# One layer with a linear recurrence on one core: keys loaded once, and the output of a pair of chunks given to the scheduler before the front of the next

## The chip, the cores and the metric

The kernel runs on one core of a Trainium2 chip. The core has a matrix engine (TensorE, in the profile PE, with its weight loads as PEld), a vector engine (VectorE, DVE), an engine for activations and copies (ScalarE, ACT), a general engine (GpSimd, POOL) and an engine that here only issues DMA transfers (SyncE, SP). Each engine works through its own queue in order; engines wait for each other through semaphores. Data lie in device memory (DRAM), in the on-chip SBUF of 128 partitions, and in PSUM, where TensorE writes its products, in banks of 512 float32 values a partition.

The metric is the device time of one execution in microseconds (us): less is better. Before the change the median of three runs is 2554.62 us, from 2553.71 to 2556.13.

## The reference

One layer of a streaming encoder for 2048 tokens of width 1024, all in float32: token mixing, cross-attention into 256 memory tokens, and a feed-forward part, each between norms. Token mixing has one input projection, whose columns go to two groups of heads: a sliding-window attention and a gated linear recurrence. The change is in the recurrence, four heads of 128 by 128 state, in chunks of 64 tokens:

```python
    f = lbf + (1.0 - lbf) * jax.nn.sigmoid(f_logit.astype(f32))
    kf = 1.0 - f
    logf = jnp.log(f)
    b = jnp.cumsum(lc, axis=3)                       # within a chunk
    A = jnp.einsum('bhnqd,bhnkd->bhnqk', qc * jnp.exp(b - b_mid), kc * jnp.exp(b_mid - b))
    A = jnp.where(causal, A, 0.0)
    o_intra = jnp.einsum('bhnqk,bhnkv->bhnqv', A, vc)
    kv = jnp.einsum('bhnkd,bhnkv->bhndv', kc * jnp.exp(b_last - b), vc)
    # S_t = decay * S_{t-1} + kv, one chunk after the other
    o_inter = jnp.einsum('bhnqd,bhndv->bhnqv', qc * jnp.exp(b), S_prev)
    o = rms_norm(o_intra + o_inter, onorm_g) * jax.nn.silu(g)
```

Then follow the output projection, the cross-attention and the feed-forward part, which fill the time from about 790 us on.

## The kernel before

**Stages.** The input projection writes its result to DRAM (`z_d`), in two halves of 1024 tokens. The recurrence reads it back in pairs of chunks, 128 tokens at a time, 16 pairs in all. Pairs 0 to 7 run in a first pass beside the window attention (`swa`) and the input projection of the second half (`in_proj`, loop over `next(swa)`, `next(hgrn)`, `next(cols)`). Pairs 8 to 15 run in a second pass: the first step near the end of the attention, the others beside `fold_cross`, which multiplies the cross-attention's weights with each other and with the memory tokens; each step of the recurrence is followed by two steps of the fold. The results of both groups of heads go to `y_d`, which the output projection reads later, block after block of 256 tokens.

**One pair** goes through four functions.

- `hgrn_front` loads the keys twice (`k1` and `kk`, both 128x512), the queries (`qq`) and the values (`v`). GpSimd makes a scaled copy of the second chunk's queries (L890). TensorE multiplies keys with queries, eight matmuls into two banks (L897); VectorE and ScalarE take them out under the causal mask into `at` (L898, L899). GpSimd scales the queries for the state (`q6`, L902; the profile calls it q) and, in place, half of the second copy of the keys (`kk`, L905). TensorE transposes `kk` (L908) and `v` (L913) into a bank each, and ScalarE copies them to `kt` and `vt` (L910, L915).
- `hgrn_state` multiplies `kt` with `vt` (L924), GpSimd decays the old state into a new tile (L925), VectorE adds (L926). It returns the state from before.
- `hgrn_out` loads the gate (`sg`), adds `at` times values and queries times the earlier state in one bank (L936, L937), ScalarE sums the squares (L941), GpSimd makes the norm's factor of them (L943, L945: a power), and VectorE multiplies it on (L946), which frees the bank.
- `hgrn_last` transposes the normed output (L954), VectorE applies gain and gate (L955), and SP stores it.

`hgrn` is the loop over them. A step of it gives, in this order: the state of the last pair, the front of the next pair, the last part of the pair before the last, and the output of the last pair.

**Buffers.** `k1`, `kk`, `v` and `kt` have one buffer each, `qq`, `q6`, `at`, `vt` and the state `W` two. In the first pass all banks of the recurrence are the two of kind "h"; in the second, the kinds "g" and "t" with two each: state, first half of the attention products, key transposes and last part take "g", the second half, the value transposes and the output take "t". The fold uses "s" and "h".

**What sets the order.** The program is given to a scheduler, which follows a time line of its own and hands each engine its instructions in the order in which it expects them to be ready; of several that are ready it takes the one given first. So the order in the program is a priority, and a load is issued as soon as its buffer is free. On the chip each queue then runs strictly in that order. All loads and stores here go through `load` and `store`, on SP's queue (L75, L78).

Of the kernel before, what the change touches and what calls it, by code (L numbers as in the profile page):

```python
# [15 lines left out]
ALU = mybir.AluOpType  # L16
AX = mybir.AxisListType

P = 128
# [14 lines left out]
C_KA, C_VA, C_QH, C_FH, C_IH, C_GH = 512, 640, 768, 1280, 1792, 2304  # L34
# [14 lines left out]
class Layer:  # L49
# [144 lines left out]
    def mix(self):  # L194
        tc, I = self.tc, self.I
        kw = dict(reuse_waits="tile")
        with contextlib.ExitStack() as left:
# [18 lines left out]
            with tc.tile_pool(name="sw", bufs=1, side="right", **kw) as self.sw:  # L216
                self.zero_tiles()
                swa = self.swa(range(NT), lambda n: "st" if n < NPB else "sth")
                hgrn = self.hgrn(range(NPB), "h")
                cols = self.in_proj(1, u)  # L220
                next(cols)
                for _ in range(NPB + 1):
                    next(swa)
                    next(hgrn)
                    next(cols)
                for _ in hgrn:
                    pass
                self.out_sums, side = self.sums("out_s", self.w_out, 4, lambda: self.io_tile("u"), lambda: self.io_tile("x"))
                side = side()
                next(side)  # L230
                pairs = self.hgrn(range(NPB, NT), "gt")
                for i, _ in enumerate(swa, NPB + 2):
                    next(cols)
                    if i == NT + 1 - 0:
                        next(pairs)
                    for _ in range(4):
                        next(side, None)
# [168 lines left out]
    def zero_tiles(self):  # L406
# [19 lines left out]
        self.vst_prev = None  # L426
        self.W = ph.tile([P, 4, P], F32, tag="W", name="W0", bufs=2)
        nc.gpsimd.memset(self.W, 0.0)

# [437 lines left out]
    def hgrn_front(self, n, kinds):  # L867
        nc, ph = self.nc, self.hg
        t0 = n * P
        z = self.z_d  # L870
        kinds = itertools.cycle(kinds)

        def get(t, c):
            self.load(t, z[c:c + 512, t0:t0 + P].rearrange("(h p) t -> p h t", p=P))
            return t

        def new(tag, bufs=1, w=P):
            return ph.tile([P, 4, w], F32, tag=tag, name=f"{tag}{n}", bufs=bufs)

        def c8(ap):  # L880
            return ap.rearrange("p h (c t) -> p (h c) t", t=64)

        k1 = get(new("k1"), C_FH)
        qq = new("qq", 2, 192)
        q1 = get(qq[:, :, 0:P], C_QH)
        kk = get(new("kk"), C_FH)
        v = get(new("v"), C_IH)
        g1 = self.G1[:, n, :].unsqueeze(2).broadcast_to([P, 4, 64])

        nc.gpsimd.tensor_tensor(qq[:, :, P:192], qq[:, :, 64:P], g1, ALU.mult)  # L890

        at = self.atz[n % 2]
        for i in range(2):
            ps = self.bank(next(kinds))[:, 0:384].rearrange("p (h t) -> p h t", h=2)
            hs = slice(2 * i, 2 * i + 2)
            for r in range(2):
                nc.tensor.matmul(ps[:, r, :], k1[:, 2 * i + r, :], qq[:, 2 * i + r, :], start=True, stop=True)  # L897
            nc.vector.copy_predicated(at[:, hs, :], self.cmask.unsqueeze(1).broadcast_to([P, 2, P]), ps[:, :, 0:P])  # L898
            nc.scalar.activation(at[0:64, hs, 64:P], ps[0:64, :, P:192], AF.Copy)  # L899

        q6 = new("q6", 2)
        nc.gpsimd.tensor_tensor(q6.rearrange("p h (c t) -> p h c t", t=64), q1.rearrange("p h (c t) -> p h c t", t=64),  # L902
                                self.G[:, n, :, :].unsqueeze(3).broadcast_to([P, 4, 2, 64]), ALU.mult)

        nc.gpsimd.tensor_tensor(kk[:, :, 0:64], kk[:, :, 0:64], g1, ALU.mult)  # L905
        ps = self.bank(next(kinds))
        for h in range(4):
            nc.tensor.transpose(ps[:, h * P:(h + 1) * P], kk[:, h, :], self.ident)  # L908
        kt = new("kt")
        nc.scalar.activation(kt, ps.rearrange("p (h t) -> p h t", h=4), AF.Copy)  # L910
        ps = self.bank(next(kinds))
        for h in range(4):
            nc.tensor.transpose(ps[:, h * P:(h + 1) * P], v[:, h, :], self.ident)  # L913
        vt = new("vt", 2)
        nc.scalar.activation(vt, ps.rearrange("p (h t) -> p h t", h=4), AF.Copy)  # L915
        return q6, at, kt, vt

    def hgrn_state(self, n, kinds, kt, vt):
        nc, ph = self.nc, self.hg
        prev = self.W  # L920
        W = self.W = ph.tile([P, 4, P], F32, tag="W", name=f"W{n}", bufs=2)
        ps = self.bank(kinds[0])
        for h in range(4):
            nc.tensor.matmul(ps[:, h * P:(h + 1) * P], kt[:, h, :], vt[:, h, :], start=True, stop=True)  # L924
        nc.gpsimd.tensor_tensor(W, prev, self.G[:, n, :, 1].unsqueeze(2).broadcast_to([P, 4, P]), ALU.mult)  # L925
        nc.vector.tensor_tensor(W, ps.rearrange("p (h t) -> p h t", h=4), W, ALU.add)  # L926
        return prev

    def hgrn_out(self, n, kinds, q6, at, vt, W):
        nc, ph = self.nc, self.hg  # L930
# [28 lines left out]
    def hgrn(self, pairs, kinds):  # L959

        f, o = {}, {}
        for n in itertools.chain(pairs, (None, None)):
            if f:
                m, (q6, at, kt, vt) = f.popitem()
                W = self.hgrn_state(m, kinds, kt, vt)
            else:
                m = None
            if n is not None:
                f[n] = self.hgrn_front(n, kinds)
            if o:  # L970
                l, v = o.popitem()
                self.hgrn_last(l, kinds, *v)
            if m is not None:
                o[m] = self.hgrn_out(m, kinds, q6, at, vt, W)
            yield

    def swa(self, pairs, kinds):
# [826 lines left out]
```

## Time and profile before

| what | value |
| --- | --- |
| median of three runs | 2554.62 us |
| the profiled execution | 2553.56 us |
| its span, first to last instruction | 2551.9 us |
| mean granted clock of TensorE | 0.998 |
| DMA traffic | 486.33 MB |
| keys, second copy (`kk`) | 16 loads of 256 KB, median 4.3 us from issue to landing |

The profile is that of one execution. A row of a time line has the start and the duration in us, the engine, the line of the kernel, the operation, what it writes and reads, and in brackets how long the engine had stood idle just before and what released it. A row of the waits has the engine and line that waited, what for, and the sum in us, the number of times and the longest. A row of the stretches has from and to, the length, the busy time of PE, PEld, DVE, ACT and POOL (with the number of instructions), the granted clock, the busy share of the DMA engines and GB/s. Names of tiles stand without their numbers: `k1` is k, `q6` is q, `at` is atz.

### The profile page before, as it was taken

Reading aid. Unit: us, or ns where it says so; the run is one execution under the profiler, and the core shown is the slowest. Engines: PE = TensorE matmul, PEld = TensorE weight load, DVE = VectorE, ACT = ScalarE, POOL = GpSimd, SP = SyncE. Lnnn points to the kernel's source line nnn. Section 1 sums busy time; section 2 is a strip of 40 time slices with the busy share of each in tenths; the row PEclk is TensorE's granted clock in tenths of the full one; section 3 lists DMA queues with packets and bytes.
Section 4 is the critical chain, followed back from the end, with each engine's and each line's share of the span. In section 5 each row is a group of like instructions: output and inputs, shape, how many; then the busy total and the mean of one; then the engine's idle time right before and its main releaser. Section 6 shows DMA issues by size and latency. Waiting matters only on the chain.

```text
span 2551.9 us, 34333 instructions
## 1 busy us (share of the span) xinstructions
PE 2505.4 (98%) x12006; PEld 2093.8 (82%) x12006; DVE 1792.5 (70%) x2871; ACT 1262.2 (49%) x2635; POOL 365.1 (14%) x540
## 2 busy tenths in 40 slices
PE   9999999999999999999999999999999999999998
PEld 8878888878897787878878888888888888888886
DVE  8785588986466889987876655576566557574766
ACT  5453466655465576566653333353333335443543
POOL 4231234321310111101200000000000000000022
PEclk9999999999999999999999999999999999999999
DMA  6455655864897996866964522254565434564776
GB/s 201 147 165 178 196 164 160 239 206 128 241 304 281 307 327 203 272 210 211 331 217 134 188 91 83 75 206 139 167 206 195 144 115 163 177 191 106 229 173 155
DMA packets 387885, 486.33 MB, mean 191 GB/s; under 512 B 22272, under 2 KB 283392, under 8 KB 387712
## 3 DMA queue, kind: packets, MB, share of 16 engines
q1 hardware_dynamic: 381664, 462.12, 55.9%
q0 software_dynamic: 6048, 22.02, 5.0%
q8 instruction: 94, 1.54, 0.2%
q14 instruction: 79, 0.65, 0.1%
HBM read 317.34 MB, written 166.72 MB: 190 GB/s over the span
## 4 chain that ended last, share of the span: by engine, by line
PE 51%; DVE 2%; DMA 1%; issue 1%; ACT 1%; POOL 0%; SPq 0%; DVEq 0%; POOLq 0%; ACTq 0%
PE psm L1144 17%; PE psm L1142 17%; PE psm L1143 17%; DVE T L1001 0%; DVE S L1001 0%; ACT junk L1517 0%; PE pss L1403 0%; DMA out_dram<-row 0%; DMA row<-in_w_down_dram 0%; DMA row<-d_s 0%; DMA sraw<-in_w_gate_dram 0%; DVE sum L1117 0%; DMA u_s<-row 0%; ACT S L998 0%; ACT T L998 0%
## 5 line engine op out<-in xcount | busy, mean ns | idle before, releaser
L1142 PE MATMUL psm<-T,S 128*128 128x512 f32 x2680 | 1035.5, 391 | 13.3 <-ACT part L1157 7.3
L1143 PE MATMUL psm<-T,S 128*128 128x512 f32 x2680 | 1043.7, 390 | 3.8 <-DVE T L1001 3.7
L1144 PE MATMUL psm<-T,S 128*128 128x512 f32 x2680 | 1031.0, 390 | 4.8 <-DVE S L1001 4.8
L1142 PEld LDWEIGHTS psm<-T,S 128*128 128x128 f32 x2680 | 503.5, 188 | 126.2 <-ACT part L1157 11.9
L1144 PEld LDWEIGHTS psm<-T,S 128*128 128x128 f32 x2680 | 503.4, 188 | 112.0 <-DVE S L1001 7.7
L1143 PEld LDWEIGHTS psm<-T,S 128*128 128x128 f32 x2680 | 503.6, 188 | 110.3 <-DVE T L1001 6.6
L998 ACT ACTIVATE S<-sum 128x512 fp32r<-128x512 f32 (+1 forms) x370 | 223.7, 619 | 377.8 <-PE psm L1144 278.5
L1001 DVE TENSOR_TENSOR S<-sraw,S 128x512 fp32r<-128x512 f32 (+1 forms) x315 | 211.8, 681 | 210.5 <-ACT S L998 207.4
L1157 ACT ACTIVATE part<-psm 128x512 f32<-128x512 f32 x285 | 168.6, 596 | 251.5 <-PE psm L1144 232.9
L1001 DVE TENSOR_TENSOR S<-sum,S 128x512 fp32r<-128x512 f32 (+1 forms) x388 | 258.0, 675 | 41.6 <-ACT S L998 37.9
L998 ACT ACTIVATE S<-sraw 128x512 fp32r<-128x512 f32 (+1 forms) x300 | 185.0, 618 | 108.4 <-PE psm L1144 105.7
L1550 POOL DMA_DIRECT2D y_d<-row x16 | 14.0, 877 | 1077.3 <-DVE row L1734 1027.7
L1001 DVE TENSOR_TENSOR T<-row,T 128x1024 fp32r<-128x1024 f32 (+1 forms) x112 | 131.4, 1186 | 28.9 <-ACT T L998 27.0
L157 PE MATMUL psg<-u,whi 128*128 128x512 f32 x320 | 127.4, 398 | 0.0
L158 PE MATMUL psg<-u,wlo 128*128 128x512 f32 x320 | 127.2, 398 | 0.0
L156 PE MATMUL psg<-u,whi 128*128 128x512 f32 x320 | 127.1, 397 | 0.0
L1517 ACT ACTIVATE junk<-row 128x512 f32<-128x512 f32 x160 | 99.6, 624 | 44.2 <-DVE row L1539 19.8
L998 ACT ACTIVATE T<-row 128x1024 fp32r<-128x1024 f32 (+1 forms) x112 | 113.3, 1031 | 8.4 <-DMA row<-d_s 4.9
L1685 DVE TENSOR_TENSOR row<-psm,part 128x512 f32<-128x512 f32 x66 | 43.7, 688 | 66.0 <-PE psm L1144 65.9
L1694 DVE TENSOR_TENSOR part<-psm,part 128x512 f32<-128x512 f32 x66 | 43.8, 688 | 60.0 <-PE psm L1144 59.9
L1734 DVE TENSOR_TENSOR row<-psm,part 128x512 f32<-128x512 f32 x72 | 49.2, 689 | 49.4 <-PE psm L1144 49.3
L825 ACT ACTIVATE S<-S,w_mn 128x256 f32<-128x256 f32 (+1 forms) x128 | 63.1, 496 | 29.9 <-DVE w_mn L821 29.6
(363 smaller groups left out, 3569.4 us busy)
## 6 DMA issues: line engine op xcount, KB each, us to landing
sraw<-in_w_gate_dram SPq DMA_DIRECT2D x44, 512.0 KB, 3.6
sraw<-in_w_up_dram SPq DMA_DIRECT2D x44, 512.0 KB, 3.7
hid_d<-row SPq DMA_DIRECT2D x44, 512.0 KB, 2.6
sraw<-hid_d SPq DMA_DIRECT2D x32, 512.0 KB, 4.4
sraw<-in_w_in_dram SPq DMA_DIRECT2D x44, 256.0 KB, 4.0
z_d<-pair SPq DMA_DIRECT2D x20, 512.0 KB, 3.4
raw<-in_w_in_dram SPq DMA_DIRECT2D x20, 512.0 KB, 5.2
z_d<-z SPq DMA_DIRECT2D x20, 512.0 KB, 3.9
```

The source lines that it names most:

```text
L156: nc.tensor.matmul(ps, ah, bh, start=(i == 0), stop=False)
L157: nc.tensor.matmul(ps, ah, bl, start=False, stop=False)
L158: nc.tensor.matmul(ps, al, bh, start=False, stop=(i == n - 1))
L825: nc.scalar.activation(s[:, r, o:], s[:, r, o:], AF.Exp, bias=mn[:, i:i + 1], scale=-1.0, accum_out=den[:, i:i + 1])
L998: self.nc.scalar.activation(hi, raw, AF.Copy)
L1001: self.nc.vector.tensor_tensor(lo, raw, f32(hi), ALU.subtract)
L1142: nc.tensor.matmul(ps, s[:, 0, k, :], t[:, 0, k, :], start=st, stop=False, **kw)
L1143: nc.tensor.matmul(ps, s[:, 0, k, :], t[:, 1, k, :], start=False, stop=False, **kw)
L1144: nc.tensor.matmul(ps, s[:, 1, k, :], t[:, 0, k, :], start=False, stop=sp, **kw)
L1157: nc.scalar.activation(t, ps, AF.Copy)
L1517: self.nc.scalar.activation(junk, a, AF.Square, scale=float(D) ** -0.5, accum_out=to)
L1734: nc.vector.tensor_tensor(d, a, b, ALU.add)
```

## The change

In `hgrn_front` the second copy of the keys is gone. `k1` gets two buffers in place of one, and after the attention products have read it, its first half of each head is scaled in place and transposed for the state. In `hgrn`, a step now gives the last part first, then the output of the last pair, then its state, then the front of the next pair. The output takes the state from `self.W` before `hgrn_state` replaces it, so nothing is returned any more.

```diff
-        k1 = get(new("k1"), C_FH)
+        k1 = get(new("k1", 2), C_FH)
         qq = new("qq", 2, 192)
         q1 = get(qq[:, :, 0:P], C_QH)
-        kk = get(new("kk"), C_FH)
         v = get(new("v"), C_IH)
...
-        nc.gpsimd.tensor_tensor(kk[:, :, 0:64], kk[:, :, 0:64], g1, ALU.mult)
+        nc.gpsimd.tensor_tensor(k1[:, :, 0:64], k1[:, :, 0:64], g1, ALU.mult)
         ps = self.bank(next(kinds))
         for h in range(4):
-            nc.tensor.transpose(ps[:, h * P:(h + 1) * P], kk[:, h, :], self.ident)
+            nc.tensor.transpose(ps[:, h * P:(h + 1) * P], k1[:, h, :], self.ident)
...
-        return prev
...
         for n in itertools.chain(pairs, (None, None)):
-            if f:
-                m, (q6, at, kt, vt) = f.popitem()
-                W = self.hgrn_state(m, kinds, kt, vt)
-            else:
-                m = None
-            if n is not None:
-                f[n] = self.hgrn_front(n, kinds)
             if o:
                 l, v = o.popitem()
                 self.hgrn_last(l, kinds, *v)
-            if m is not None:
-                o[m] = self.hgrn_out(m, kinds, q6, at, vt, W)
+            if f:
+                m, (q6, at, kt, vt) = f.popitem()
+                o[m] = self.hgrn_out(m, kinds, q6, at, vt, self.W)
+                self.hgrn_state(m, kinds, kt, vt)
+            if n is not None:
+                f[n] = self.hgrn_front(n, kinds)
             yield
```

## The prediction

> **What bounds the kernel now.** I read the page first (busy shares, the 40 slices), then the busy time by stretches, then who TensorE waited for, then the time line around each gap.
>
> ```profile
> span 2551.9 us, 34333 instructions
> PE 2505.4 (98%) x12006; PEld 2093.8 (82%) x12006; DVE 1792.5 (70%) x2871; ACT 1262.2 (49%) x2635; POOL 365.1 (14%) x540
> ```
>
> TensorE is the bound from end to end. The change adds and removes no matmul and no transpose, so it can act only through the 2551.9 - 2505.4 = 46.5 us in which TensorE stands idle, and through the clock. The recurrence runs in two passes: pairs 0 to 7 beside the window attention and the input projection (about 250 to 500 us), pairs 8 to 15 mostly beside the folding of the cross-attention weights (620 to 730 us). The busy time of these stretches:
>
> ```profile
> core 0: us, PE busy (x) PEld busy (x) DVE busy (x) ACT busy (x) POOL busy (x), PEclk, DMA share, GB/s
> 250.00:500.00 250.00, 248.87 (x1410) 214.85 (x1410) 190.72 (x458) 146.46 (x428) 91.88 (x142) 1.00 0.64 187
> 620.00:790.00 170.00, 161.01 (x1160) 150.61 (x1159) 83.98 (x118) 93.43 (x208) 31.49 (x41) 0.99 0.84 266
> 665.00:670.00 5.00, 2.42 (x18) 1.95 (x16) 2.63 (x4) 1.08 (x2) 2.16 (x3) 1.00 0.71 174
> 670.00:675.00 5.00, 4.78 (x42) 4.81 (x43) 2.64 (x6) 2.14 (x10) 1.39 (x2) 1.00 1.15 312
> 690.00:700.00 10.00, 6.56 (x38) 6.15 (x38) 4.30 (x7) 2.77 (x7) 3.61 (x5) 0.83 0.90 308
> 790.00:1000.00 210.00, 202.30 (x873) 164.15 (x872) 185.95 (x256) 129.41 (x287) 35.33 (x64) 0.99 0.85 284
> ```
>
> The first pass leaves 1.1 us idle: nothing to win there, only to lose. The second leaves 9.0 us, and 2.58 + 0.22 + 3.44 = 6.24 us of it lies in two places, at 665 and at 690. What held TensorE there, and what held the others (waits from 250 to 800 us for TensorE, from 520 to 790 us for the rest):
>
> ```profile
> PE pst L913 <- DVE on L946: 2.6, 1, 2.6
> PE psg L908 <- issue: 1.4, 1, 1.4
> PE pst L913 <- ACT whi L126: 1.4, 1, 1.4
> PE psg L908 <- ACT atz L899: 0.3, 1, 0.3
> ...
> POOL qq L890 <- DMA qq<-z_d: 58.2, 7, 12.1
> DVE on L946 <- POOL h_rs L945: 20.8, 7, 8.3
> ```
>
> The time line at 690, all engines:
>
> ```profile
> 687.10 0.22 ACT L941 ACTIVATION_READ_ACCUMULATOR on<-pst 128x1 f32 x1
> 688.97 0.61 POOL L890 TENSOR_TENSOR qq<-qq,G 128x256 f32<-128x256 f32 x1 [10.76 <-DMA qq<-z_d]
> 689.80 0.61 POOL L905 TENSOR_TENSOR kk<-kk,G 128x256 f32<-128x256 f32 x1 [0.22 <-PE psh L124]
> 690.37 1.05 POOL L925 TENSOR_TENSOR W<-W,G 128x512 f32<-128x512 f32 x1
> 691.37 1.04 POOL L902 TENSOR_TENSOR q<-qq,G 128x512 f32<-128x512 f32 x1
> 692.50 0.19 POOL L943 TENSOR_SCALAR h_vv<-h_ss 128x4 f32<-128x4 f32 x1
> 692.77 1.01 POOL L945 TENSOR_TENSOR h_rs<-h_vv,mhalf 128x4 f32<-128x4 f32 x1
> 693.82 0.69 DVE L946 TENSOR_TENSOR on<-pst,h_rs 128x512 f32<-128x512 f32 x1 [8.28 <-POOL h_rs L945]
> 694.56 0.66 PE L913 MATMUL pst<-ident,v 128*128 128x128 f32 x4 [2.60 <-DVE on L946]
> ```
>
> ScalarE has the sums of squares of one pair's output ready at 687.3. GpSimd takes them up at 692.5, because its queue holds ahead of them the query scaling L890 of a later pair, which waits 10.76 us for a load, and then three operations of the next pair's front and state. VectorE stands still for 8.28 us on the normalisation L946, and the value transposes L913 need the PSUM bank that L946 frees. At 665 it is the same chain, smaller:
>
> ```profile
> 662.57 0.61 POOL L890 TENSOR_TENSOR qq<-qq,G 128x256 f32<-128x256 f32 x1 [6.76 <-DMA qq<-z_d]
> ...
> 667.37 0.69 DVE L946 TENSOR_TENSOR on<-pst,h_rs 128x512 f32<-128x512 f32 x1 [4.04 <-POOL h_rs L945]
> 668.16 0.63 PE L913 MATMUL pst<-ident,v 128*128 128x128 f32 x4 [1.37 <-ACT whi L126]
> 669.44 0.68 DVE L926 TENSOR_TENSOR W<-psg,W 128x512 f32<-128x512 f32 x1
> 670.22 0.63 PE L908 MATMUL psg<-ident,kk 128*128 128x128 f32 x4 [1.44 <-issue]
> ```
>
> L913 starts 0.10 us after L946 ends (667.37 + 0.69 = 668.06), though the row names ScalarE; L908 starts 0.10 us after the state sum L926, which VectorE made late because it had stood on L946. And the clock, microsecond by microsecond after the second gap:
>
> ```profile
> 696.00:697.00 1.00, 0.70 (x3) 0.71 (x4) 1.00 (x3) 0.00 (x0) 0.00 (x0) 0.67 0.84 287
> 697.00:698.00 1.00, 1.00 (x7) 1.00 (x6) 1.00 (x3) 0.18 (x1) 0.00 (x0) 0.50 0.98 393
> 698.00:699.00 1.00, 1.00 (x6) 1.00 (x6) 0.12 (x1) 0.21 (x2) 0.00 (x0) 0.50 1.04 364
> 699.00:700.00 1.00, 1.00 (x8) 1.00 (x7) 0.00 (x0) 0.98 (x3) 0.00 (x0) 0.63 1.07 329
> ```
>
> The lost clock is 0.33 + 0.50 + 0.50 + 0.37 = 1.7 us. Idle and clock together: 6.24 + 1.7 = 7.9 us.
>
> **The change, part by part.**
>
> *Output ahead of state and front.* Now L943 and L945 of the finished pair are given before L925, L890, L902 and the key scaling of the next. In the gap at 690 that takes 0.61 + 1.05 + 1.04 = 2.7 us from ahead of L943, which is just the 2.60 us that TensorE stood; at 665 the same three durations are more than the 1.37 us. What is late next: the wait of L890 for its load stays where readiness puts it, ahead of all of them. But in both gaps it ended (688.97 and 662.57) before TensorE came to the next attention products (those at 690.9, a row below, end 2 us after it), and the output products now stand at the head of the step, so their sums need GpSimd only 1.95 + 1.26 = 3.2 us later (rows below). I take the whole 7.9 us as recovered; ends 0 and 7.9. The output's load (sg) and the store of the previous pair now go ahead of the front's loads on SP's queue; no row of TensorE's waits between 250 and 800 us names a load, so this costs 0 while the loads stay a pair ahead, and it is the landing of qq that it would delay.
>
> A cost comes with it. The value transposes of a pair wait for the bank of the output just given, in the same step and no longer in the one before. From the first output matmul to the free bank lie, from rows above and these,
>
> ```profile
> 684.11 0.38 PE L936 MATMUL pst<-vt,atz 128*128 128x128 f32 x2
> 685.67 0.39 PE L937 MATMUL pst<-W,q 128*128 128x128 f32 x2
> ```
>
> 1.95 us of matmuls, 1.26 us of squares (686.06 to 687.32), 1.3 us of GpSimd (L943, L945), 0.7 us of VectorE: 5.2 us. State, attention products and fold matmuls cover it; if they run out, up to 8 pairs stand 2.6 us (the worst gap) = 20.8 us. I take 1.5 us, near the lower end, since TensorE waited for such banks 2.6 + 1.4 us in all in this pass.
>
> *Keys loaded once.*
>
> ```profile
> kk<-z_d SPq DMA_DIRECT2D x16, 256.0 KB, 4.3
> L905 POOL TENSOR_TENSOR kk<-kk,G x16: 612/613/1594, 269.5 to 704.0; 128x256 f32<-128x256 f32 x16
> ```
>
> Sixteen loads of 256 KB go, 4.2 MB, with their places on SP's queue. TensorE waited for none, so 0; queues that run at a share of 0.84 get some relief, which I leave in the lower end. The key tile has two buffers and its load can start a pair earlier: 0 as well.
>
> *Scaling in place.* GpSimd now waits for the four attention products that read the keys, and the key transposes L908 for GpSimd: a hop of about 0.1, 0.61 us, a hop of 0.1, so 0.8 us from the last product to the first transpose; 1.8 us at the longest duration of L905 (1594 ns). Behind the waiting instruction on GpSimd stand the next L943/L945 and, in the first pass, the weight splits. On TensorE the cover is fold and projection matmuls. Ends: 0, and 16 x 0.8 = 12.8 us if nothing covers it. Before, the transposes had their keys from GpSimd too and waited 1.4 + 0.3 us in all; I add as much again, 1.7 us.
>
> The Trainium skill (SBUF — State Buffer, section "SBUF: two separate sides") says that GpSimd and VectorE share one port pair under an exclusive lock, so an operation of either can be held for the whole of the other's. The longest L905 agrees (1594 against 613 ns), and its median shows how seldom. By the page alone each scaling could be held, and the sum would lose up to 16 us more; by the rows it loses one microsecond once.
>
> *Afterwards.* From 790 to 1000 us TensorE stands idle 7.7 us with VectorE at 89% and DMA at 0.85: work that arrives earlier may be given back there. 0; ends -2 and +4.
>
> **Sum:** -7.9 + 1.5 + 1.7 = -4.7 us on the profiled 2553.56 us, 2548.9. The median of the runs, 2554.62, is 1.06 us above the profiled one, so 2549.9.
>
> On the clock the Trainium skill (TensorE: Matmul & The Clock Gate, "What's actually happening") says that TensorE falls to half rate after an idle window of about 3.4 us, whose phase is free. The trace agrees: half clock after 690, none after the shorter gap at 665. By that rule the 1.7 us go whole even if a microsecond of the gap stays; by a share of the idle time, a gap cut in half would give only half of them.
>
> **The rivals.**
>
> *Slower.* The in-place scaling sits in GpSimd's queue behind L890 of the next pair, which waits for its late load; the key transposes then stand in TensorE's queue. In favour: L890 waited 58.2 us in seven pairs. Against: L890 was free before the products ended, by 654.94 - 650.26 = 4.7 us and 691.72 - 688.97 = 2.8 us in two steps:
>
> ```profile
> 650.26 0.61 POOL L890 TENSOR_TENSOR qq<-qq,G 128x256 f32<-128x256 f32 x1 [10.61 <-DMA qq<-z_d]
> 654.13 0.81 PE L897 MATMUL pst<-qq,k 128*128 128x192 f32 x4
> 690.91 0.81 PE L897 MATMUL pst<-qq,k 128*128 128x192 f32 x4
> ```
>
> It decides when the earlier keys let the products run some 3 us sooner against that load. A pair then costs 2.6 us and the clock 1.7; three such pairs, 12.9 us, make -4.7 + 12.9 = +8.2: 2562.8 us.
>
> *Nothing moves.* The scheduler orders each queue by when it believes work ready; L890 stays ahead, the stalls remain or only wander: 2554.6 us. In favour: the first 10.76 us of the wait at 690 are that load's. Against: the last 2.7 us are not.
>
> *More than forecast.* New waits cost 0, and with fewer loads the rest of the second pass's idle time, 9.0 - 6.24 = 2.75 us, goes too: -10.65, so 2544.0 us. Against: that rest has other releasers.
>
> **How the numbers follow.** Forecast 0.48, slower 0.22, nothing moves 0.20, more 0.10. A measurement tells 0.2%, 5.1 us, from no change, and the forecast of -4.7 lies at that bound: of its 0.48 I count 0.26 faster, 0.20 same, 0.02 slower (its own range 2546 to 2556). Nothing-moves gives 0.18 same and 0.02 slower. Faster 0.26 + 0.10 = 0.36, same 0.38, slower 0.26. The range runs from 2543, a microsecond under the largest gain, to 2564, just above the slower rival.
>
> **What would show it.** Right: no idle of L913 on L946 and no dip of the clock in the second pass; the wait of L946 for L945 falls far under 20.8 us; L943 directly behind L890 and not behind L925 and L902; the 16 kk loads gone; TensorE's wait at L908 under 4 us. Wrong: L908 waiting for GpSimd over several pairs, L913 waiting on L946 in most pairs, idle time in the first pass above 3 us, or a gap that only moves to 790 to 1000 us.

## The result, and the profile after

The changed kernel takes 2551.01 us (median, 2544.8 to 2557.95), the kernel before 2553.84 us (2548.6 to 2558.13) on the same chips. The ratio is 0.9985 with a 95% interval of 0.9979 to 0.9991: 3.8 us are gained, between 2.3 and 5.4 us (the two medians as they stand lie 2.8 us apart). The prediction had -4.7 us and 2549.9 us.

The span of the changed kernel's profile is 2549.8 us. Its busy times:

```profile
PE 2504.8 (98%) x12006; PEld 2094.9 (82%) x12006; DVE 1794.9 (70%) x2871; ACT 1261.8 (49%) x2635; POOL 372.7 (15%) x540
```

As before, TensorE has 12006 matmuls and about 2505 us of work; 45 us of idle time remain, 1.5 us less than before. The profiled execution itself took 2551.48 us against 2553.56 before, so the two traces show 2.1 of the 3.8 us.

Stretches of the changed kernel (columns: length, busy time of TensorE, its weight loads, VectorE, ScalarE and GpSimd, granted clock, DMA share, GB/s):

```profile
250.00:500.00 250.00, 247.85 (x1408) 214.41 (x1406) 195.09 (x470) 150.69 (x441) 95.36 (x144) 1.00 0.60 173
500.00:620.00 120.00, 117.30 (x624) 98.75 (x624) 97.91 (x242) 67.55 (x186) 26.23 (x42) 0.99 0.62 191
620.00:700.00 80.00, 79.86 (x630) 77.54 (x628) 37.44 (x58) 40.86 (x112) 28.96 (x35) 1.00 0.74 220
700.00:790.00 90.00, 85.37 (x538) 76.54 (x537) 46.53 (x57) 50.26 (x93) 4.06 (x6) 0.98 0.85 290
790.00:1000.00 210.00, 201.49 (x876) 163.40 (x875) 186.81 (x261) 130.53 (x290) 36.46 (x65) 1.00 0.86 281
```

The kernel before had in three of these, and from 660 to 710 us, where its two gaps lie:

```profile
500.00:620.00 120.00, 117.76 (x617) 97.92 (x616) 96.69 (x248) 68.53 (x192) 25.63 (x45) 1.00 0.57 177
620.00:700.00 80.00, 72.86 (x577) 70.94 (x576) 37.99 (x60) 38.90 (x104) 23.87 (x31) 0.98 0.80 232
700.00:790.00 90.00, 88.15 (x585) 79.67 (x584) 45.99 (x58) 54.53 (x105) 7.62 (x10) 1.00 0.87 296
660.00:710.00 50.00, 43.75 (x350) 42.90 (x349) 21.05 (x34) 25.15 (x71) 17.09 (x23) 0.97 0.83 247
```

From 620 to 700 us the idle time fell from 7.14 to 0.14 us and the clock stayed whole: 7.0 us of idle time and 1.7 us of clock are recovered, a little more than the 7.9 us of the forecast's first step. From 700 to 790 us it rose from 1.85 to 4.63 us, with a dip of the clock: 2.8 + 1.7 = 4.5 us are given back there. Elsewhere 1.0 us more is idle in the first pass (2.15 against 1.13), 0.5 us more from 500 to 620 and 0.8 us more from 790 to 1000 (8.5 against 7.7). The clock dips there too. The changed kernel has a dip from 595 to 599 us and one from 1107 to 1111 us (0.57 in both), the kernel before one from 887 to 891 us, each of 1.7 us again:

```profile
595.00:599.00 4.00, 4.00 (x19) 3.37 (x17) 4.00 (x11) 2.02 (x5) 0.00 (x0) 0.57 0.76 262
887.00:891.00 4.00, 4.00 (x12) 3.12 (x12) 3.48 (x5) 0.14 (x1) 0.88 (x1) 0.57 1.08 333
```

So over the whole execution the idle time is 1.5 us less, and the changed kernel has one dip more (three against two, without the last 8 us, which run at half clock in both). Idle time and clock do not add up to the 2.1 us between the two executions. What the traces show directly is the lead: the last matmul on the fold's output weights (L361) starts at 772.1 us, before at 775.0, so 2.9 us are gained by then, and 0.8 us are lost again behind it. A microsecond of one trace is little evidence in any case: up to 250 us all kernels of this document have the same order on every queue, and TensorE's idle time there is between 7.1 and 9.7 us.

The waits of the changed kernel, TensorE's from 250 to 800 us, the others' from 520 to 790 us (line waited on, releaser; total, times, longest):

```profile
PE pss L359 <- ACT whi L993: 3.5, 1, 3.5
PE psh L912 <- ACT atz L898: 0.3, 1, 0.3
POOL qq L889 <- DMA qq<-z_d: 32.4, 7, 6.2
DVE on L944 <- POOL h_rs L943: 6.6, 2, 4.0
```

Lines behind the front have moved up by one or two: L890 of before is L889, L902 is L901, L905 is L904, L908 is L907, L913 is L912, L925 is L924, L937 is L935, L943, L945 and L946 are L941, L943 and L944, L998 is L993. No wait of the value transposes on the normalisation is left; the normalisation waits 6.6 us for its factor where it waited 20.8; query scaling waits 32.4 us for its load where it waited 58.2. One wait is new and costs 3.5 us, that of L359, which belongs to the fold of the output weights.

The time line at 690 us, the place of the worst gap of before:

```profile
689.94 0.61 POOL L889 TENSOR_TENSOR qq<-qq,G 128x256 f32<-128x256 f32 x1 [6.18 <-DMA qq<-z_d]
690.26 0.38 PE L935 MATMUL pst<-W,q 128*128 128x128 f32 x2
690.72 1.04 POOL L901 TENSOR_TENSOR q<-qq,G 128x512 f32<-128x512 f32 x1 [0.17 <-PE pst L935]
691.98 0.19 POOL L941 TENSOR_SCALAR h_vv<-h_ss 128x4 f32<-128x4 f32 x1 [0.22 <-ACT on L939]
692.26 1.01 POOL L943 TENSOR_TENSOR h_rs<-h_vv,mhalf 128x4 f32<-128x4 f32 x1
693.67 0.68 DVE L944 TENSOR_TENSOR on<-pst,h_rs 128x512 f32<-128x512 f32 x1
693.83 1.04 POOL L924 TENSOR_TENSOR W<-W,G 128x512 f32<-128x512 f32 x1 [0.57 <-DVE W L925]
695.52 0.61 POOL L904 TENSOR_TENSOR k<-k,G 128x256 f32<-128x256 f32 x1 [0.65 <-PE pst L896]
696.15 0.60 PE L912 MATMUL pst<-ident,v 128*128 128x128 f32 x4
```

From the end of the last output product to the normalisation it is now 693.67 - 690.64 = 3.0 us; before it was 693.82 - 686.06 = 7.8 us. The state's scaling L924 and the key scaling L904 have moved behind the factor. The query scalings L889 and L901 have not: they still stand ahead of L941. The value transposes L912 come 1.8 us after the normalisation has freed their bank, and wait for nothing.

The new gap is at 744 us. The matmul behind it and the ScalarE operation that released it:

```profile
746.91 1.06 ACT L993 ACTIVATE whi<-raw 128x1024 fp32r<-128x1024 f32 x1 [1.80 <-DMA raw<-in_wo_x_dram]
748.01 0.50 PE L359 MATMUL pss<-whi,kv 128*128 128x512 f32 x1 [3.54 <-ACT whi L993]
```

ScalarE splits an output weight of the fold that has only just landed. The DMA issues on SyncE's queue (start, length of the issue, transfer, number), first of the changed kernel:

```profile
730.88 0.58 SPq L78 DMA_DIRECT2D y_d<-sg  x1
...
733.47 2.69 SPq L75 DMA_DIRECT2D sraw<-y_d  x4
736.25 4.86 SPq L75 DMA_DIRECT2D raw<-in_wo_x_dram  x3
```

and of the kernel before:

```profile
736.32 1.97 SPq L78 DMA_DIRECT2D y_d<-sg  x1
...
742.11 0.34 SPq L75 DMA_DIRECT2D raw<-in_wo_x_dram  x1
742.54 3.16 SPq L75 DMA_DIRECT2D sraw<-y_d  x4
```

The recurrence's last store is out 5.4 us earlier. Soon after it the output projection's first four token reads (512 KB each) are issued, and three of the fold's output weights, which TensorE needs at once, go behind them. Before, one of these weight loads went first. So part of the gain is given back, as the prediction feared, but right behind the recurrence and not at 790 to 1000 us.

### The profile page after: what moved, and what is told of

Read it like the earlier page. It is cut to its first block, busy times and chain, and to the rows that moved or that the text cites. A ratio compares the mean times of both kernels' runs of the same rounds, so it can differ in the third digit from the quotient of the medians.

```text
span 2549.8 us, 34301 instructions
## 1 busy us (share of the span) xinstructions
PE 2504.8 (98%) x12006; PEld 2094.9 (82%) x12006; DVE 1794.9 (70%) x2871; ACT 1261.8 (49%) x2635; POOL 372.7 (15%) x540
## 4 chain that ended last, share of the span: by engine, by line
PE 80%; DVE 7%; DMA 6%; ACT 3%; issue 3%; POOL 1%; SPq 1%; DVEq 0%; POOLq 0%; ACTq 0%
PE psm L1137 22%; PE psm L1139 22%; PE psm L1138 22%; PE psg L158 2%; PE psg L157 2%; PE psg L156 2%; DVE T L996 1%; DMA h1t_d<-row 1%; DVE S L996 1%; ACT junk L1512 1%; DMA raw<-in_wv_x_dram 1%; SPq L75 1%; DVE row L1406 1%; DVE sum L1112 0%; DMA qd<-z_d 0%
## 5 line engine op out<-in xcount | busy, mean ns | idle before, releaser
L993 ACT ACTIVATE S<-sum 128x512 fp32r<-128x512 f32 (+1 forms) x370 | 223.5, 619 | 378.1 <-PE psm L1139 276.3
L993 ACT ACTIVATE S<-sraw 128x512 fp32r<-128x512 f32 (+1 forms) x300 | 185.0, 618 | 113.1 <-PE psm L1139 110.3
L993 ACT ACTIVATE T<-row 128x1024 fp32r<-128x1024 f32 (+1 forms) x112 | 113.3, 1031 | 5.7 <-DMA row<-d_s 3.5
L996 DVE TENSOR_TENSOR wlo<-raw,whi 128x1024 fp32r<-128x1024 f32 x44 | 53.8, 1223 | 44.6 <-ACT whi L993 29.5
```

Source lines behind the costliest of these rows:

```text
L993: self.nc.scalar.activation(hi, raw, AF.Copy)
L996: self.nc.vector.tensor_tensor(lo, raw, f32(hi), ALU.subtract)
```

## The experiments

Two theories stood at the start. *Queue:* the order of the step alone makes the gain, since it takes the state's and the keys' operations from ahead of the output's small ones on GpSimd; the saved loads are worth nothing (as predicted). *Loads:* the gaps come from late loads, and what helps is that sixteen of them go. Each kernel is compared with runs of the kernel before on the same chip.

**Order alone.** The changed kernel with the second key load and its own tile left in.

```diff
-        k1 = get(new("k1", 2), C_FH)
+        k1 = get(new("k1"), C_FH)
+        kk = get(new("kk"), C_FH)
-        nc.gpsimd.tensor_tensor(k1[:, :, 0:64], k1[:, :, 0:64], g1, ALU.mult)
+        nc.gpsimd.tensor_tensor(kk[:, :, 0:64], kk[:, :, 0:64], g1, ALU.mult)
-            nc.tensor.transpose(ps[:, h * P:(h + 1) * P], k1[:, h, :], self.ident)
+            nc.tensor.transpose(ps[:, h * P:(h + 1) * P], kk[:, h, :], self.ident)
```

> The new order of the steps alone; the keys are still loaded twice, one buffer each. Queue theory (the norm's factor of a finished pair no longer stands behind the next pair's GpSimd work): both gaps of the second pass go, TensorE idle under 1 us between 660 and 700 us, no wait of L913 on L946 over 1 us, time 0.9985 of before. Load theory (the gain came from sixteen fewer loads, so the queries landed sooner): at least one gap of 2 us or more stays between 660 and 700 us, the query scaling waits over 50 us for its loads in the second pass as before, time 1.000.

Measured: 2559.13 us, ratio 1.0024 (1.0013 to 1.0035). It is slower than before. Its waits from 520 to 790 us, and the stretch of the gaps:

```profile
POOL qq L890 <- DMA qq<-z_d: 35.1, 6, 6.9
POOL kk L905 <- DMA kk<-z_d: 28.0, 6, 12.8
DVE on L945 <- POOL h_rs L944: 16.8, 6, 3.8
...
660.00:710.00 50.00, 45.63 (x365) 44.25 (x364) 22.83 (x37) 24.56 (x71) 17.82 (x24) 0.97 0.90 271
```

4.4 us of idle time and the clock's dip stay (6.25 us in the same 50 us before). GpSimd now stands 28.0 us on the second key load, and the normalisation still 16.8 us on its factor. The queue theory's forecast fails. Two gaps of 1.9 and 1.6 us at 678 and 706 us end with the normalisation. GpSimd has the key scaling ahead of the factor there, and starts it 0.13 and 0.14 us after the second key load has landed (675.61 and 703.53 us). The loss against the kernel before comes ahead of the gaps: 3.5 us are idle from 250 to 500 us (1.1 before) and 5.1 from 500 to 620 (2.2 before), and the clock dips four times up to 1000 us, at 392, 539, 679 and 757 us (0.57 over 4 us each), where before it dipped twice.

**Keys alone.** The kernel before, old order, with the keys loaded once into two buffers and scaled in place.

```diff
-        k1 = get(new("k1"), C_FH)
+        k1 = get(new("k1", 2), C_FH)
-        kk = get(new("kk"), C_FH)
-        nc.gpsimd.tensor_tensor(kk[:, :, 0:64], kk[:, :, 0:64], g1, ALU.mult)
+        nc.gpsimd.tensor_tensor(k1[:, :, 0:64], k1[:, :, 0:64], g1, ALU.mult)
-            nc.tensor.transpose(ps[:, h * P:(h + 1) * P], kk[:, h, :], self.ident)
+            nc.tensor.transpose(ps[:, h * P:(h + 1) * P], k1[:, h, :], self.ident)
```

> The keys loaded once and scaled in place, the steps in the old order. Queue theory: the norm's factor still stands behind the next pair's front and state, so L946 keeps waiting for it 15 to 25 us in the second pass, at least one gap of 2 us stays, time 1.000 (0.999 to 1.002). Load theory: the queries land in 3 to 4 us in place of 5, the gaps go, time 0.9985.

Measured: 2552.95 us, ratio 0.9998 (0.9989 to 1.0006), no change. The stretches that tell:

```profile
500.00:620.00 120.00, 113.96 (x593) 92.55 (x592) 97.95 (x255) 71.12 (x197) 25.32 (x44) 1.00 0.59 180
660.00:710.00 50.00, 49.36 (x413) 48.96 (x412) 25.46 (x43) 27.27 (x78) 19.95 (x25) 1.00 0.81 248
```

The gaps are gone without any change of the order, and GpSimd's wait for the queries from 520 to 790 us falls from 58.2 to 22.0 us. But 6.0 us are idle from 500 to 620 us, where before it was 2.2, and the time stays. That stretch is the end of the window attention; TensorE's waits there are on its probabilities (VectorE, ScalarE).

**Keys alone, one buffer.** The same with `new("k1")`.

> The old order of the step with the keys loaded once, scaled in place, and one key buffer; beside the run with two buffers (ratio 0.9998, no gap left in the second pass but 6.0 us idle from 500 to 620 us instead of 2.2). If the earlier key loads of the second buffer disturbed the tail of the window attention, this run has under 3.5 us idle from 500 to 620 us and a ratio of about 0.9985. If loads and order act only together, whatever the buffer, it stays at 0.9990 to 1.0005.

Measured: 2558.81 us, ratio 1.0015 (1.0005 to 1.0025). The second buffer did not disturb the window attention; without it the same stretch is worse:

```profile
500.00:620.00 120.00, 112.85 (x588) 92.56 (x588) 94.94 (x249) 70.97 (x198) 25.87 (x45) 0.99 0.56 168
```

So loading the keys once, in the old order, takes most of the gaps at 665 and 690 us away (0.6 and 2.0 us idle from 660 to 710 us, 6.25 before), and the time does not fall. From 500 to 620 us 3.8 and 4.9 us are lost again; why there, and where the rest goes, was not found.

**The change with one key buffer.** `new("k1", 2)` becomes `new("k1")`.

> The changed kernel with one buffer for the keys in place of two, so the load of a pair's keys waits until the last pair's keys are transposed; sixteen loads fewer than before and the new order stay. If the prefetch that the second buffer allows is what makes the two parts work together, the attention products wait for late keys, gaps come back between 640 and 710 us (TensorE idle 2 us and more there) and the time is 1.000 to 1.003 of before. If the missing loads are what counts, it stays at 0.9985 to 0.999.

Measured: 2550.37 us, ratio 0.9979 (0.9970 to 0.9988). In the new order the second buffer is not needed: the gap that was expected came (TensorE stands 2.7 us on key loads between 640 and 710 us), the longer time did not. Set beside the old order with one buffer (1.0015), the order is worth 0.36% once the keys are loaded once: the intervals lie apart. With two buffers it is 0.13% (0.9998 and 0.9985), and the intervals overlap.

**A load that nobody reads.** The change with the second key load put back, into a tile that is never used.

```diff
+        get(new("kk"), C_FH)
         v = get(new("v"), C_IH)
```

> The changed kernel with the second load of the keys put back, into a tile that nobody reads: the 4.2 MB and sixteen places on SP's queue return, the order, the two buffers and the scaling in place stay. If relief of the queues and of SP is the gain, the time goes back to 1.000 and above, with the query scaling waiting 45 us and more for its loads in the second pass. If the prefetch and the order are the gain, it stays at 0.9985 to 0.9992 and 620 to 700 us stays without a gap of 2 us.

Measured: 2552.36 us, ratio 0.9999 (0.9990 to 1.0007). By this ratio the gain is gone; the interval just touches that of the change, and the plain medians (2554.91 us for the kernel before) differ by 0.10%. The gaps do not come back (79.86 us busy of 80 from 620 to 700 us, as in the changed kernel), and the query scaling waits about as long for its load (31.8 against 32.4 us).

But these loads are not where the removed ones were. Nobody reads their tile, so its buffer is free as soon as a load has landed. Their issues, and those of the run below whose second load is read:

```profile
L75 SPq DMA_DIRECT2D kk<-z_d x16: 359/371/3112, 265.1 to 554.9; - x16
L75 SPq DMA_DIRECT2D kk<-z_d x16: 371/522/1730, 264.2 to 706.7; - x16
```

The eight of the second pass all go between 508 and 555 us, and none is under way from 620 to 730 us. The order changed as well: up to 1000 us 62 of TensorE's 5223 instructions and 48 of VectorE's 1346 stand elsewhere in their queues. Nor is the loss tied to the time of the loads. In the traces this run is 2.0 us behind the change at the last L361 (774.1 against 772.1 us), 0.6 us at about 1030 us and 3.3 us at about 1150 us. In between lies a gap of 2.3 us at 1041 us that the change does not have, with a dip of the clock behind it (0.57 from 1044 to 1048 us). So this run does not show what the bytes of the loads cost.

**An eighth of that load.** Same place in the program, 64 pieces of 512 bytes instead of 512.

```diff
+        spare = new("kk")
+        self.load(spare[0:16], z[C_FH:C_FH + 64, t0:t0 + P].rearrange("(h p) t -> p h t", p=16))
         v = get(new("v"), C_IH)
```

> The changed kernel with a load of an eighth of the keys (64 packets of 512 bytes instead of 512) at the place of the loads that the change removed; it computes the whole reference. With the whole load put back the ratio was 0.9999, without it 0.9985. If what the sixteen loads cost is their bytes and packets, this run stands near the change, 0.9985 (2550 us). If it is the place of an instruction on SP's queue ahead of the values' load, it stands near 0.9999 (2553.5 us).

Measured: 2548.92 us, ratio 0.9980 (0.9971 to 0.9988), as fast as the change. Its interval and that of the whole load (0.9990 to 1.0007) lie apart. So sixteen more issues on SyncE's queue cost nothing that can be measured. These loads too go early (263.8 to 387.3 us), and up to 1000 us GpSimd's 402 instructions and SyncE's other 654 transfers stand in the order of the change. So the two runs differ in the bytes, in when they are moved, and in the order of the other work; which of these sets them apart is not shown.

**The second load's scaling put behind the factor.** Order alone, but the scaling of the second key load stands on GpSimd behind the output's factor, where the scaling in place stands in the changed kernel.

```diff
         nc.gpsimd.tensor_tensor(rs, vv, self.mhalf[:, 0:4], ALU.pow)
+        self.rs_at = self.traced(mybir.EngineType.Pool)
...
-        nc.gpsimd.tensor_tensor(kk[:, :, 0:64], kk[:, :, 0:64], g1, ALU.mult)
+        with self.queued(*([self.rs_at] if self.rs_at is not None else [])):
+            nc.gpsimd.tensor_tensor(kk[:, :, 0:64], kk[:, :, 0:64], g1, ALU.mult)
```

> The new order of the step with the keys still loaded twice (ratio 1.0024 alone, the normalisation waiting 16.8 us for its factor from 520 to 790 us), but the scaling of the second key load put behind the last norm factor on GpSimd's queue, where the scaling in place stands in the changed kernel. If the order alone failed because the scaling of the early key load stands ahead of the output's small operations on GpSimd, that wait falls under 9 us, 660 to 710 us has under 2 us idle, and the ratio comes down to that of the changed kernel with the spare load, about 0.9999 (2553.5 us). If it failed because of what the loads carry, the wait and the ratio stay near 16 us and 1.002 (2558 us).

Measured: 2558.78 us, ratio 1.0018 (1.0008 to 1.0027). Waits from 520 to 790 us and the stretch of the gaps:

```profile
POOL kk L907 <- DMA kk<-z_d: 18.8, 5, 13.0
DVE on L948 <- POOL h_rs L946: 10.5, 4, 6.5
PE psg L910 <- POOL kk L907: 2.0, 2, 1.8
...
660.00:710.00 50.00, 46.02 (x362) 45.31 (x362) 21.85 (x34) 25.33 (x66) 17.41 (x23) 0.93 0.84 260
```

The normalisation's wait fell from 16.8 to 10.5 us, so the place on GpSimd's queue matters; it is not what decides, since 4.0 us stay idle and the time hardly moved. GpSimd still stands on the second load, and now the key transposes wait behind it. Its bytes are those of the run with the unread load (0.9999, at most 1.0007), but it moves them later, as the rows above show. An instruction waits for them here, and 93 of SyncE's 670 transfers up to 1000 us come in another order. So how much of the second load's price is this dependency, and how much its bytes, stays open.

**Query scaling put behind the factor.** The kernel before, with L890 of a pair queued on GpSimd behind the last norm factor, so that its wait for the load holds nobody's output.

```diff
-        nc.gpsimd.tensor_tensor(qq[:, :, P:192], qq[:, :, 64:P], g1, ALU.mult)
+        with self.queued(*([self.rs_at] if self.rs_at is not None else [])):
+            nc.gpsimd.tensor_tensor(qq[:, :, P:192], qq[:, :, 64:P], g1, ALU.mult)
```

> The kernel before, with the query scaling of a pair put behind the norm's factor of the pair two earlier on GpSimd; order of steps and both key loads as before. If the wait of the query scaling for its load was what made the norm's factor late, the gaps at 665 and 690 us go here too, without either part of the change: TensorE idle under 1.5 us there, L946 waits under 8 us for the factor, 0.9975 to 0.999 of before. If the other three operations in front of the factor were the cause, L946 still waits 15 us and more, a gap of 1 us or more stays, and the time is 1.000 within 0.001.

Measured: 2561.82 us, ratio 1.0035 (1.0021 to 1.0049). Two waits from 520 to 790 us:

```profile
DVE on L949 <- POOL h_rs L947: 5.1, 5, 1.2
PE psg L899 <- POOL qq L892: 4.5, 1, 4.5
```

The wait for the factor is all but gone, and the attention products stand instead on the query scaling that comes too late. The load's lateness now holds up another instruction.

**Twice the scaling.** The change with one more pass over all the keys on GpSimd (a multiplication by 1), between the scaling in place and the key transposes.

```diff
         nc.gpsimd.tensor_tensor(k1[:, :, 0:64], k1[:, :, 0:64], g1, ALU.mult)
+        nc.gpsimd.tensor_scalar(k1, k1, 1.0, 1.0, ALU.mult, ALU.mult)
```

> The changed kernel with one more GpSimd pass over all of the keys (128x512, times 1) between the scaling in place and the transposes: some 1 us more on the way from the attention products to the key transposes, in each of 16 pairs. If that way is covered by other matmuls, as its price of 0 to 1.7 us in the prediction assumed, the time stays within 2 us of the changed kernel (0.9978 to 0.9993 of before). If it is open, up to 16 us come on top: 1.003 to 1.005.

Measured: 2551.49 us, ratio 0.9986 (0.9977 to 0.9995), not told apart from the change, though each pair has one operation more, of 618 ns in the median and 1471 at the longest. No cost of the longer way from the last attention product to the key transposes shows, within 0.1%; 366 of TensorE's instructions up to 1000 us also changed their place, so the comparison is not of this operation alone.

**The fold's weights first.** The change, with the output projection's first four token reads queued on SyncE behind the third output-weight load.

```diff
+                if j == 2:
+                    self.wo_at = self.traced(mybir.EngineType.SP)
...
+            with self.queued(*([self.wo_at] if n < 4 else [])):
+                self.load(t, src[n:n + 2, :, 512 * j:512 * j + 512].rearrange("i p c -> p i c"))
```

> The changed kernel, with the output projection's first four reads of the mixed tokens queued on SP behind the third load of the cross-attention's output weights; nothing else. If the gap of 3.5 us at 743 us comes from the 2 MB of token reads that now go ahead of those weights, it goes with its clock dip (1.7 us): 4 to 5 us less than the changed kernel, 2546.5 us, 0.997 of before. If the weights are late because the DMA queues are full at that place whatever the order, the gap moves or stays and the time is that of the changed kernel, 0.9985 of before, within 1 us.

Measured: 2550.54 us, ratio 0.9993 (0.9984 to 1.0002); not told apart from the change. The gap is smaller, 2.5 us, and ends some 5 us later:

```profile
753.26 0.50 PE L361 MATMUL psh<-whi,kv 128*128 128x512 f32 x1 [2.54 <-DVE kv L315]
```

Now VectorE holds it: it splits token blocks, whose reads come later, ahead of the last of the fold's projected values (L315).

**And the splits behind the fold's last values.** The same, with the first token splits queued on ScalarE and VectorE behind the last L315.

```diff
+        self.kv_at = [self.traced(e) for e in (mybir.EngineType.Activation, mybir.EngineType.DVE)]
...
+            with self.queued(*(() if first else self.kv_at)):
+                upto(need[i])
```

> wo_first with the splits of the output projection's first token blocks also put behind the last split of the fold's projected values on ScalarE and VectorE. If the 2.5 us gap that wo_first left at 753 us comes from VectorE standing on a late token block ahead of that split, the gap and its clock dip (1.7 us) go: 4 us less than wo_first, 0.9970 to 0.9978 of before. If the fold's end is short of ready matmuls anyway, or the output projection now starts late by as much, the time stays at 0.9985 to 0.9995.

Measured: 2548.94 us, ratio 0.9981 (0.9972 to 0.9990).

**Both, with one key buffer.**

> The change with one key buffer (ratio 0.9979 alone) and with the output projection's first token reads and their splits held behind the fold's third output-weight load and the last split of its keys and values (0.9981 alone). If what the two give adds up, 0.9975 (2547.5 us); if both only show the scatter of the planner's orders around the change, 0.9980 to 0.9985.

Measured: 2548.47 us, ratio 0.9975 (0.9967 to 0.9984), the lowest of all. From 700 to 790 us it has

```profile
700.00:790.00 90.00, 89.29 (x582) 80.59 (x581) 48.99 (x61) 54.44 (x100) 4.30 (x7) 1.00 0.92 321
```

0.7 us idle where the change has 4.6, and a full clock: the gap at 744 us can be avoided. It beats the kernel before; against the change (0.9979 to 0.9991) the intervals overlap, so a gain in time is not shown.

The runs that carry the argument, side by side:

| order of the step | key loads | ratio to before | interval |
|---|---|---|---|
| old | once, two buffers | 0.9998 | 0.9989 to 1.0006 |
| old | once, one buffer | 1.0015 | 1.0005 to 1.0025 |
| new | twice, second one read | 1.0024 | 1.0013 to 1.0035 |
| new | twice, read behind the factor | 1.0018 | 1.0008 to 1.0027 |
| new | twice, second one unread | 0.9999 | 0.9990 to 1.0007 |
| new | once and an eighth unread | 0.9980 | 0.9971 to 0.9988 |
| new | once, one buffer | 0.9979 | 0.9970 to 0.9988 |
| new | once, two buffers (the change) | 0.9985 | 0.9979 to 0.9991 |

Neither half gains alone; the two together do. In the new order the second load, when it is read, costs 0.33 to 0.45% (1.0018 and 1.0024 against 0.9985 and 0.9979), well clear of the intervals. What it is about that load stays open. A rival for all small differences is the scheduler: each edit changes its order of other work as well, and the kernels that keep the change and add an edit of their own lie between 0.9975 and 0.9999. So a difference of 0.15% or less cannot be put down to one edit here.

## Why the prediction was right in the sum, and where its steps failed

*Output ahead of state and front, -7.9 us.* The size was right: 7.0 us idle and 1.7 us of clock went from 620 to 700 us. The cause was half right. The step said that the order takes 2.7 us from ahead of L943, and that this is what TensorE stood for. The order alone left 4.4 of 6.25 us, and the keys alone closed the gaps in the old order. Of the three durations that it counted as removed (L905, L925 and L902), L902's 1.04 us (now L901) still stand ahead of the factor; what moved behind is the state's scaling and the keys'. And the whole term of the order, -7.9 + 1.5 = -6.4 us, is not what the order does: alone it measured 0.24% slower, 6.1 us.

*Sixteen loads, 0.* This is the step that failed: "TensorE waited for none, so 0". In the new order taking the second load out turned 1.0024 into 0.9985 (0.9979 with one buffer), about 10 us; in the old order it was worth nothing (0.9998, and 1.0015 with one buffer). So the term has no price of its own: it depends on the order of the step, and the prediction added the two. TensorE did not wait for the load, but GpSimd did, and its queue is in order. In the kernel before this happened twice from 520 to 790 us:

```profile
593.47 0.61 POOL L905 TENSOR_TENSOR kk<-kk,G 128x256 f32<-128x256 f32 x1 [9.78 <-DMA kk<-z_d]
704.01 0.61 POOL L905 TENSOR_TENSOR kk<-kk,G 128x256 f32<-128x256 f32 x1 [10.23 <-DMA kk<-z_d]
```

Neither wait lies at the gaps of 665 and 690 us, so the rows of before did not give the price away. With the new order alone there are six such waits, 28.0 us, and behind the key scaling stands the norm's factor: the two gaps that are left there, at 678 and 706 us, come of it. That this makes the whole 10 us is not shown: with the scaling put behind the factor, 1.0018 remained.

*Value transposes on the bank of the same step, +1.5 us.* In the trace 0: TensorE has no wait of L912 on the normalisation; at 690 us the output's chain takes 3.0 us, and the transposes come 1.8 us after it.

*Scaling in place, +1.7 us.* About 0: L904 waits 8.2 us for the products from 520 to 790 us, no row of TensorE there waits for it, and with the extra pass no cost was seen. The prediction weighed the Trainium skill (SBUF — State Buffer, "SBUF: two separate sides"), by which each scaling could be held by a VectorE operation; the extra pass had a median of 618 ns and a longest of 1471. The longest, at 277.9 us, ran beside a VectorE split (277.6 to 278.9 us), which agrees; the median shows that most were not held.

*Afterwards, 0.* 4.5 us were given back at 744 us. From 790 to 1000 us 0.8 us more are idle, and one dip of the clock less. The mechanism (work that arrives earlier) was right, its place wrong, and its size about the end of +4 that the step allowed: 4.5 + 0.8 = 5.3 us, or 3.6 with that dip counted.

The near hit of the sum, -4.7 against -3.8 us, is luck in good part. The runs do not split the gain into the prediction's terms: the order that should bring -6.4 us brings +6.1 alone, the keys that should cost 1.7 cost about 0 alone, and both together give -3.8, so some 10 us come from the two edits acting together, which no term held. The 4.5 us given back at 744 us, which the sum had at 0, then took part of that away.

The rivals: the slower one (key scaling behind a late query load) did not occur, L907 has no wait. Of "nothing moves", the part that the query scaling stays ahead came true. "More than forecast" came true from 620 to 700 us only: 8.7 us went there where 7.9 were forecast.

## What to carry to other kernels

A load for which the bottleneck engine never waits need not be free: look for every in-order engine that does wait for it, and for what will stand behind that wait in the new order. Two edits to one loop can each be worth nothing and a gain together, so their terms cannot be priced one by one and added; split them on the chip before keeping one half. A load that nobody reads is no stand-in for one that is read, since it goes out as soon as its buffer is free: look in the trace at when it was issued. And when a stage ends earlier, ask which queued transfers its memory lets go, and whether they now go ahead of one that is needed sooner.

## What the runs showed of the hardware

A dip of the clock cost about the same 1.7 us behind gaps of different length. Behind the gap of 3.54 us in the changed kernel (microsecond by microsecond, the clock in the column before the DMA share):

```profile
748.00:749.00 1.00, 0.97 (x3) 0.49 (x3) 1.00 (x1) 0.82 (x1) 0.00 (x0) 0.97 1.04 385
749.00:750.00 1.00, 0.72 (x2) 0.63 (x3) 0.95 (x2) 1.00 (x3) 0.00 (x0) 0.50 0.38 139
750.00:751.00 1.00, 1.00 (x4) 0.81 (x3) 1.00 (x3) 0.52 (x1) 0.00 (x0) 0.50 0.68 152
751.00:752.00 1.00, 1.00 (x4) 0.71 (x3) 0.96 (x1) 0.00 (x0) 0.00 (x0) 0.50 0.93 365
752.00:753.00 1.00, 1.00 (x5) 0.85 (x4) 0.00 (x0) 0.00 (x0) 0.00 (x0) 0.83 1.05 180
```

0.03 + 0.50 + 0.50 + 0.50 + 0.17 = 1.7 us, as after the 2.60 us gap of before. With the fold's weights first, the gap of 2.54 us was followed by 0.52, 0.50, 0.50 and 0.77, again 1.7 us. So a gap that was shortened from 3.5 to 2.5 us kept the whole dip. The prediction weighed the Trainium skill on this (TensorE: Matmul & The Clock Gate, "What's actually happening"): half rate after an idle window of about 3.4 us. By that rule the loss goes or stays as a whole. That is what these runs show. As for the length, 2.5 us of continuous idle time were enough there, and the dip at 595 us in the changed kernel came after gaps of 0.93, 0.34 and 0.57 us within 3 us; but with the unread load a gap of 2.48 us at 749 us left the clock at 1.00. So the length of the gap alone does not decide.
